# S5 outputs of a hybrid encoder as 64x64 matmul tiles by direction, with one copy of the states per tile

## The chip, the core and the metric

The kernel runs on one core of one Trainium2 chip. The metric is the time of one execution on the device in microseconds (us). TensorE (PE; its weight loads PEld) does the matmuls, VectorE (DVE) and ScalarE (ACT) the elementwise work, GpSimd (POOL) a little, and SyncE (SP) issues the DMAs.

## The reference

Two layers over 256 positions of width 2048. Each projects the stream, sends one half through a bidirectional complex-diagonal state space model (S5) in 64 groups of 16 channels with 64 states per direction, the other half through differential attention, and adds the projection of both back, followed by a LayerNorm. What matters here is the SSM:

```
for direction in range(2):
    y = y + s5_scan(uf, lam[direction], ..., b[direction], c[direction], reverse=(direction == 1))
# s5_scan: x_t = a * x_{t-1} + B u_t (complex, associative scan along time), returns
    einsum('bsgp,gcp->bsgc', x_re, c_re) - einsum('bsgp,gcp->bsgc', x_im, c_im)
```

The backward direction runs over time reversed, so its states come out in the opposite order of time.

## The kernel before

The weights (512 KB pieces) stream through SP's queue into `raw`, four deep. Each piece is split into a high part `wh` (a cast on ACT, L163) and a low part `wl` (a subtraction on VectorE, L165), and a **step** of 24 matmuls (`mm3`, L169 to L171) multiplies it. After every step the program calls `side`, which lets generators ("lanes") emit pieces of the SSM and of the attention heads; a scheduler then sets each engine's order when the program is built. All engines work through their order one instruction after the other.

The SSM runs in blocks of four positions: 64 blocks, the scan (`ssm_scan`, L552 to L555) over them on VectorE in `H`, whose innermost index is not the block. Partitions 0 to 63 of `H` hold the forward states, 64 to 127 the backward ones, whose blocks are in reversed order. `ssm_out` then goes through eight **tiles** o of eight groups. For a tile:

- `part` (L457, L459) builds the weights `w` from the table and C on VectorE, six operations;
- ACT copies the tile's states from `H` into `hcs` (names in the profile: `bh`), contiguous in blocks: the forward half as it is (L629), the backward half read in reverse (L630);
- `expand` (L571, `kw`) and `toep` (L578 on TensorE, L583 on ACT) make the local kernel `lt` inside a block;
- `outputs` (L592, L595) multiplies: per pair of groups pr, and for re and im, the two groups g2 with 128 states (both directions at once) by 64 outputs, and `lt` by U over 128 rows of which half are zero. One PSUM bank (`ss`, two in the pool) takes the tile; ACT copies it into `y4s` (`ub`, L599);
- every second tile `ready` stores y to memory; `load_y` and `split_y` read it back transposed, apply GELU (L617) and split it for the next matmuls.

Two tiles' `w` and two tiles' `hcs` exist at a time, and one `lt`. In both layers the tiles run beside the steps of the gate's projection (silu, L926) and of the output projection's first half. Parameters of the emission order (`BUDGET`, `PE_SHARE`, the costs that the lanes yield) are the same before and after.

Of the kernel before, what the change touches and what calls it, by code (L numbers as in the profile page):

```python
# [43 lines left out]
def kernel(  # L44
# [28 lines left out]
    V, A, PE, GP, SY = nc.vector, nc.scalar, nc.tensor, nc.gpsimd, nc.sync  # L73
    mult, add, sub = ALU.mult, ALU.add, ALU.subtract
# [4 lines left out]
    def T(shape, tag, bufs=1, dt=F32):  # L79
        return sb.tile(shape, dt, tag=tag, name=tag, bufs=bufs)  # L80

    def PS(shape, tag, bufs):
        return pp.tile(shape, F32, tag=tag, name=tag, bufs=bufs)

    def tp_bank(shape):
        return PS(shape, "tp", 2)

    def ss_bank(shape):
        return PS(shape, "ss", 2)
# [303 lines left out]

    cz = [T([128, 2, 8, 32], f"cz{i}") for i in range(2)]
    lt = [T([128, 8, 16, 4], f"lt{i}") for i in range(1)]
    for t in cz + lt:
        GP.memset(t, 0.0)

    class Ssm:
# [51 lines left out]
    def part(w, z, o, tr, M, m0, m1, op, r):  # L451

        gs = slice(8 * o, 8 * o + 8)
        x2 = T([128, 8, 16, 4], "x2")
        for dst, a, m in ((x2, tr + 1, m1), (w[:, r], tr, m0)):
            t = z.tab[:, a, 32 * o:32 * o + 32].rearrange("p (g j) -> p g j", j=4)
            V.tensor_tensor(dst, t.unsqueeze(2).to_broadcast([128, 8, 16, 4]),  # L457
                            M[:, m, gs, :].unsqueeze(3).to_broadcast([128, 8, 16, 4]), mult)
        V.tensor_tensor(w[:, r], w[:, r], x2, op)  # L459
# [98 lines left out]
    def ssm_out(l):  # L558
        z = ssm[l]
        y4s = {}  # L560
        hcs = T([128, 2, 2, 2, 4, 64], "bh")
        z.yT = z.yh = None
        ws = {}
        kws = {}

        def expand(o):

            kw = kws[o] = T([128, 2, 4, 16, 4], "kw")
            for q in range(2):
                w0 = z.kx[:, 2 * o + q, :, 3:7]  # L570
                A.copy(kw[:, q], bass.AP(w0.tensor, w0.offset, [w0.ap[0], [-1, 4], *w0.ap[1:]]))  # L571

        def toep(o):
            kw = kws[o]
            lp = tp_bank([128, 4, 64])
            for j in range(4):
                for q in range(2):
                    PE.matmul(lp[64 * q:64 * q + 64, j], lhsT=kw[:, q, j].rearrange("p c j -> p (c j)"), rhs=sel,  # L578
                              start=True, stop=True)
            for q in range(2):  # L580
                lv = lp[64 * q:64 * q + 64].rearrange("p j (a b c) -> p b a c j", a=2, b=2)
                for g2 in range(2):
                    A.copy(lt[0][64 * g2:64 * g2 + 64, 4 * q + g2:4 * q + 4:2], lv[:, g2])  # L583

        def outputs(o):
            yp = ss_bank([128, 4, 64])
            w, hc = ws[o], hcs[:, o % 2]
            for pr in range(4):
                halves = [(2 * pr + g2, yp[64 * g2:64 * g2 + 64, pr, :]) for g2 in range(2)]
                for ri in range(2):  # L590
                    for g, dst in halves:
                        PE.matmul(dst, lhsT=w[:, ri, g].rearrange("p c j -> p (c j)"),  # L592
                                  rhs=hc[:, g // 4, ri, g % 4, :], start=ri == 0, stop=False, skip_group_check=True)
                for g, dst in halves:
                    PE.matmul(dst, lhsT=lt[0][:, g].rearrange("p c j -> p (c j)"),  # L595
                              rhs=z.U[:, 4 * o + pr, :], start=False, stop=True, skip_group_check=True)
            if o % 2 == 0:
                y4s[o // 2] = T([128, 8, 64], "ub", 2)
            A.copy(y4s[o // 2][:, 4 * (o % 2):4 * (o % 2) + 4, :], yp)  # L599

        yv = y_dr.rearrange("(q g c) (j k) -> (g c j) q k", g=2, c=16, j=4)

        def ready(n):
            SY.dma_start(yv[:, 8 * n:8 * n + 8], y4s[n])

        def load_y():
            z.yT = T([128, 8, 256], "a8", 3)
            for n in range(2):
                SY.dma_start(z.yT[:, 4 * n:4 * n + 4],
                             y_dr[512 * n:512 * n + 512].rearrange("(o p) t -> p o t", p=128))  # L610

        def split_y():
            z.yh = T([128, 8, 256], "bh", 1, F32R)
            z.yl = T([128, 8, 256], "c8", 1, F32R)
            for c in range(4):
                cs = slice(2 * c, 2 * c + 2)
                A.activation(z.yT[:, cs], z.yT[:, cs], AF.Gelu_apprx_tanh)  # L617
            for c in range(4):
                cs = slice(2 * c, 2 * c + 2)
                A.copy(z.yh[:, cs], z.yT[:, cs])  # L620
                V.tensor_tensor(z.yl[:, cs], z.yT[:, cs], z.yh[:, cs].bitcast(F32), sub)

        for o in range(9):
            if o < 8:
                w = ws[o] = T([128, 2, 8, 16, 4], "w4", 2)
                part(w, z, o, 2, z.C, 0, 1, add, 0)
                hc = hcs[:, o % 2].rearrange("p q r g k -> p q (r g) k")
                src = z.H[:, 2 * o:2 * o + 2, 0:64].rearrange("p q k r g -> p q (r g) k")
                A.copy(hc[0:64], src[0:64])  # L629
                A.copy(hc[64:128], src[64:128, :, :, ::-1])  # L630
            if o > 0:
                outputs(o - 1)
                if o % 2 == 0:
                    ready(o // 2 - 1)
            if o < 8:
                expand(o)
            yield 1.8 if o < 8 else 0.0, 0, 2.5 if o else 0.0
            if o < 8:
                part(ws[o], z, o, 2, z.C, 1, 0, sub, 1)
                toep(o)  # L640
                yield 1.8, 0, 0.5
        load_y()
        yield 0.0, 2
        split_y()
        yield 2.0, 0
# [211 lines left out]
    for l in range(DEPTH):  # L857
# [8 lines left out]
        z = ssm[l]  # L866
# [30 lines left out]
        for hp in range(4):  # L897
            acc = block(hi, lo)
            while heads and heads[1].stage < 1:
                heads[1].one()  # L900
            rq = Lane(rotary_split(acc, 0.125, store, "q", (("qr", 1), ("xr", 2))), 0)
            rq.one()
            acc = block(hi, lo)
            finish(rq)
            rk = Lane(rotary_split(acc, 1.0, store, "k", (("kr", 1), ("xr", 2))), 0)
            rk.one()
            acc = block(hi, lo, tok_major=True)
            v = T([128, 2, 256], "v", 2)
            A.copy(v, acc)
            finish(rk)  # L910
            if hp == 0:
                l_out = Lane(ssm_out(l), 4, after=[l_scan])
            every += [Lane(head(hp, h, store["q"], store["k"], v, oT, neg, gsc), 1 + 0.1 * h) for h in range(2)]
            heads = every[-2:]
# [155 lines left out]
```

## Time and profile before

| | |
|---|---|
| median of 3 runs | 1031.38 us (1029.9 to 1032.72) |
| profiled execution | 1032.34 us, span 1030.6 us |
| TensorE, VectorE, ACT busy | 965.9, 773.8, 605.9 us |
| mean granted clock of TensorE | 0.985 |
| outputs stage, layer 0 and layer 1 | about 342 to 414 us and 806 to 889 us |

Busy time of TensorE counts matmuls from start to modelled end; consecutive ones overlap, so a row's busy time, not the mean of one matmul, says what a stream of them takes. "Idle before" in a row is the time in which the engine stood still ahead of it, with the instruction that ended the wait.

### The profile page before, as it was taken

What the parts mean: (1) busy time and instruction counts of PE and PEld (TensorE: products, weight loads), DVE (VectorE), ACT (ScalarE), POOL (GpSimd) and SP (SyncE); (2) the same over time, 40 slices, a digit from 0 to 9 for tenths busy, and PEclk for the clock granted to TensorE, in tenths of its full rate; (3) what the DMA queues carried; (4) which work ended last, traced back from release to release, by engine and by line L of the source; (5) the groups of instructions that cost most, each with busy time, mean ns of one, the idle gap of its engine ahead of it and who ended that gap; (6) DMA issues with size and microseconds to landing.
All of it is one profiled execution on the core that took longest, in us unless ns stands there. A gap on an engine that the chain in (4) does not pass through costs nothing.

```text
span 1030.6 us, 23623 instructions
## 1 busy us (share of the span) xinstructions
PE 965.9 (94%) x9792; PEld 932.7 (91%) x9792; DVE 773.8 (75%) x1310; ACT 605.9 (59%) x962; POOL 67.7 (7%) x104
## 2 busy tenths in 40 slices
PE   2899999999999988999889999999999998999995
PEld 2889988999999887999879989999999897999995
DVE  6875799899887666655588699988988566565676
ACT  2546586655575899444344585565566879843640
POOL 1000131010010000000010120010010000000001
PEclk9999999999999998999999999999999999999998
DMA  9897522455465524779965724545455443677973
GB/s 270 240 271 218 179 62 62 146 182 165 144 193 164 174 88 124 247 241 303 275 207 166 232 59 146 177 152 162 152 162 179 142 144 104 179 231 238 316 241 85
DMA packets 201867, 186.08 MB, mean 181 GB/s; under 512 B 38048, under 2 KB 194464, under 8 KB 201760
## 3 DMA queue, kind: packets, MB, share of 16 engines
q1 hardware_dynamic: 201760, 184.57, 58.4%
q8 instruction: 77, 1.26, 0.5%
q14 instruction: 30, 0.25, 0.1%
HBM read 169.21 MB, written 15.34 MB: 179 GB/s over the span
## 4 chain that ended last, share of the span: by engine, by line
PE 66%; ACT 11%; DMA 9%; DVE 7%; issue 3%; SPq 3%; POOL 1%; POOLq 0%; DVEq 0%; ACTq 0%
PE acc L169 19%; PE acc L170 18%; PE acc L171 18%; DMA raw<-in_w_out_dram 3%; ACT bh L630 3%; DVE wl L165 2%; ACT bh L629 2%; DMA rpart<-xr 2%; ACT wh L163 2%; PE ss L502 2%; PE sc L699 1%; PE tp L474 1%; PE ss L727 1%; PE ss L592 1%; DVE H L236 1%
## 5 line engine op out<-in xcount | busy, mean ns | idle before, releaser
L165 DVE TENSOR_TENSOR wl<-raw,wh 128x1024 fp32r<-128x1024 f32 x266 | 324.7, 1222 | 182.2 <-ACT wh L163 181.2
L163 ACT CAST wh<-raw 128x1024 fp32r<-128x1024 f32 x266 | 278.3, 1049 | 257.7 <-PE acc L170 109.6
L169 PE MATMUL acc<-xh,wh 128*128 128x256 f32 x1280 | 371.4, 291 | 2.4 <-ACT wh L163 1.3
L170 PE MATMUL acc<-xl,wh 128*128 128x256 f32 x1280 | 366.5, 286 | 3.0 <-DVE xl L254 2.9
L171 PE MATMUL acc<-xh,wl 128*128 128x256 f32 x1280 | 365.8, 286 | 1.8 <-DVE wl L165 1.8
L169 PEld LDWEIGHTS acc<-xh,wh 128*128 128x128 f32 x1280 | 246.3, 193 | 7.3 <-ACT xh L253 1.6
L170 PEld LDWEIGHTS acc<-xl,wh 128*128 128x128 f32 x1280 | 246.8, 193 | 4.9 <-DVE xl L254 4.0
L171 PEld LDWEIGHTS acc<-xh,wl 128*128 128x128 f32 x1280 | 246.7, 193 | 3.4 <-DVE wl L165 2.5
L169 PE MATMUL acc<-wh,xh 128*128 128x256 f32 x720 | 206.6, 287 | 2.7 <-ACT wh L163 1.9
L170 PE MATMUL acc<-wl,xh 128*128 128x256 f32 x720 | 205.7, 286 | 3.0 <-DVE wl L165 2.8
L171 PE MATMUL acc<-wh,xl 128*128 128x256 f32 x720 | 204.7, 285 | 0.0
L170 PEld LDWEIGHTS acc<-wl,xh 128*128 128x128 f32 x720 | 139.2, 193 | 4.1 <-DVE wl L165 4.0
L169 PEld LDWEIGHTS acc<-wh,xh 128*128 128x128 f32 x720 | 139.1, 193 | 3.7 <-ACT wh L163 2.5
L171 PEld LDWEIGHTS acc<-wh,xl 128*128 128x128 f32 x720 | 139.1, 193 | 0.1
L552 DVE TENSOR_TENSOR sa<-tab,H 128x256 f32<-128x256 f32 x126 | 53.1, 421 | 2.9 <-ACT H L505 0.7
L459 DVE TENSOR_TENSOR w<-w,x 128x512 f32<-128x512 f32 x64 | 45.5, 712 | 0.8
L709 ACT ACTIVATE e<-sc,mx 128x256 f32<-128x256 f32 x64 | 29.5, 476 | 19.3 <-DVE mx L703 19.3
L592 PE MATMUL ss<-bh,w 128*64 128x64 f32 x512 | 32.6, 236 | 6.5 <-ACT ub L599 6.5
L555 DVE TENSOR_TENSOR H<-sa 128x128 f32<-128x128 f32 x126 | 36.2, 287 | 2.1
L554 DVE TENSOR_TENSOR sa<-sa,H 128x128 f32<-128x128 f32 x126 | 36.1, 286 | 1.9
L505 ACT COPY H<-ss 128x512 f32<-128x512 f32 x32 | 33.9, 1176 | 4.1 <-PE ss L502 4.1
L171 PE MATMUL acc<-bh,wl 128*128 128x256 f32 x128 | 36.1, 282 | 0.0
(189 smaller groups left out, 1292.9 us busy)
## 6 DMA issues: line engine op xcount, KB each, us to landing
raw<-in_w_in_dram SPq DMA_DIRECT2D x192, 512.0 KB, 3.5
raw<-in_w_out_dram SPq DMA_DIRECT2D x64, 512.0 KB, 5.4
raw<-in_w_glu_dram SPq DMA_DIRECT2D x16, 512.0 KB, 5.4
xr<-xres SPq DMA_DIRECT2D x16, 256.0 KB, 3.5
rpart<-xr SPq DMA_DIRECT2D x16, 256.0 KB, 5.1
xr<-rpart SPq DMA_DIRECT2D x15, 256.0 KB, 4.6
xres<-H SPq DMA_DIRECT2D x14, 256.0 KB, 3.7
H<-in_x_dram SPq DMA_DIRECT2D x8, 256.0 KB, 5.9
```

The source lines that it names most:

```text
L163: A.copy(wh, raw)
L165: V.tensor_tensor(wl, raw, wh.bitcast(F32), sub)
L169: PE.matmul(o, lhsT=lh, rhs=rh, start=first, stop=False, skip_group_check=True)
L170: PE.matmul(o, lhsT=lh, rhs=rl, start=False, stop=False, skip_group_check=True)
L171: PE.matmul(o, lhsT=ll, rhs=rh, start=False, stop=last, skip_group_check=True)
L459: V.tensor_tensor(w[:, r], w[:, r], x2, op)
L505: A.copy(z.H[:, 2 * o:2 * o + 2, 1:65].rearrange("p q k r g -> p q (r g) k")[:, :, g2::2], ps[g2].rearrange("p q r g k -> p q (r g) k"))
L552: V.tensor_tensor(a.rearrange("p v q r g -> p v q (r g)"), lam, h.unsqueeze(1).to_broadcast([128, 2, 16, 8]), mult)
L554: V.tensor_tensor(a[:, 0], a[:, 0], nx, add)
L555: V.tensor_tensor(nx, a[:, 0], a[:, 1, :, ::-1, :], add)
L592: PE.matmul(dst, lhsT=w[:, ri, g].rearrange("p c j -> p (c j)"), rhs=hc[:, g // 4, ri, g % 4, :], start=ri == 0, stop=False, skip_group_ch ...
L630: A.copy(hc[64:128], src[64:128, :, :, ::-1])
```

## The change

Three things change in `ssm_out`, and one at the start.

1. The states are copied by one instruction for all 128 partitions, none reversed.
2. `outputs` multiplies by 64x64 tiles: row half d is the direction, column half g2 the group of the pair. Each direction has a PSUM bank of its own, and the backward states are read in reverse by the matmul. The `lt` matmuls take the diagonal quadrants alone, 64 rows each, so that the zeros in `lt` are no longer read and are no longer written at the start. A tile has 40 matmuls, not 24.
3. The result is ACT's copy of the one bank, to which VectorE adds the other.

```diff
-    for t in cz + lt:
+    for t in cz:
         GP.memset(t, 0.0)
...
         def outputs(o):
-            yp = ss_bank([128, 4, 64])
+            yps = [ss_bank([128, 4, 64]) for _ in range(2)]
             w, hc = ws[o], hcs[:, o % 2]
+            halves = [slice(0, 64), slice(64, 128)]
             for pr in range(4):
-                halves = [(2 * pr + g2, yp[64 * g2:64 * g2 + 64, pr, :]) for g2 in range(2)]
                 for ri in range(2):
-                    for g, dst in halves:
-                        PE.matmul(dst, lhsT=w[:, ri, g].rearrange("p c j -> p (c j)"),
-                                  rhs=hc[:, g // 4, ri, g % 4, :], start=ri == 0, stop=False, skip_group_check=True)
-                for g, dst in halves:
-                    PE.matmul(dst, lhsT=lt[0][:, g].rearrange("p c j -> p (c j)"),
-                              rhs=z.U[:, 4 * o + pr, :], start=False, stop=True, skip_group_check=True)
+                    for d in range(2):
+                        for g2 in range(2):
+                            g = 2 * pr + g2
+                            h = hc[halves[d], g // 4, ri, g % 4, :]
+                            PE.matmul(yps[d][halves[g2], pr, :],
+                                      lhsT=w[halves[d], ri, g].rearrange("p c j -> p (c j)"),
+                                      rhs=h[:, ::-1] if d else h,
+                                      start=ri == 0, stop=ri == 1 and d != g2, skip_group_check=True)
+                for g2 in range(2):
+                    PE.matmul(yps[g2][halves[g2], pr, :],
+                              lhsT=lt[0][halves[g2], 2 * pr + g2].rearrange("p c j -> p (c j)"),
+                              rhs=z.U[halves[g2], 4 * o + pr, :], start=False, stop=True, skip_group_check=True)
...
-            A.copy(y4s[o // 2][:, 4 * (o % 2):4 * (o % 2) + 4, :], yp)
+            y4 = y4s[o // 2][:, 4 * (o % 2):4 * (o % 2) + 4, :]
+            A.copy(y4, yps[0])
+            V.tensor_tensor(y4, y4, yps[1], add)
...
-                A.copy(hc[0:64], src[0:64])
-                A.copy(hc[64:128], src[64:128, :, :, ::-1])
+                A.copy(hc, src)
```

In the changed kernel the lines further down have other numbers: L597 and L602 are the matmuls of the states and of `lt`, L608 the copy, L609 the addition, L639 the copy of the states, L627 the GELU, L935 the silu.

The order of ACT, layer 0, one tile and the beginning of the next, before (`bh` is `hcs`, `ub` the tile's result):

```order
L629 COPY bh<-H 64x1024 [waits PE_49]
L630 COPY bh<-H 64x1024
L599 COPY ub<-ss 128x256 [waits PE_49]
L583 COPY lt_73<-tp 64x2x64 [waits PE_49,Activation_49]
L583 COPY lt_73<-tp 64x2x64 [waits Activation_49] x3
L571 COPY kw<-kx 128x256 [waits Activation_49]
L571 COPY kw<-kx 128x256
L163 CAST wh<-raw 128x1024 [waits DMAHW7_49,DVE_49,PE_49]
```

And the same place now:

```order
L639 COPY bh<-H 128x1024 [waits PE_49]
L608 COPY ub<-ss 128x256 [waits PE_49]
L583 COPY lt_73<-tp 64x2x64 [waits PE_49,Activation_49]
L583 COPY lt_73<-tp 64x2x64 [waits Activation_49] x3
L571 COPY kw<-kx 128x256 [waits Activation_49]
L571 COPY kw<-kx 128x256
L163 CAST wh<-raw 128x1024 [waits DMAHW7_49,DVE_49,PE_49]
```

One copy is gone; the rest stands as it stood.

The order of VectorE in layer 0, between two weight subtractions, before (w and x are made by `part`):

```order
L457 TENSOR_TENSOR w_4725<-tab,c_1061 128x512 [waits PE_49]
L457 TENSOR_TENSOR w_4725<-tab,c_1061 128x512
L459 TENSOR_TENSOR w_4725<-w_4725,x_4726 128x512 [waits DVE_49]
L457 TENSOR_TENSOR x_4762<-tab,c_1061 128x512 [waits DVE_49]
L459 TENSOR_TENSOR w_4725<-w_4725,x_4762 128x512 [waits DVE_49]
L457 TENSOR_TENSOR x_4780<-tab,c_1061 128x512 [waits DVE_49]
L165 TENSOR_TENSOR wl<-raw,wh 128x1024 [waits DMAHW7_49,PE_49,Activation_49]
```

And now:

```order
L457 TENSOR_TENSOR w_4740<-tab,c_1060 128x512 [waits PE_49]
L457 TENSOR_TENSOR w_4740<-tab,c_1060 128x512
L459 TENSOR_TENSOR w_4740<-w_4740,x_4741 128x512 [waits DVE_49]
L609 TENSOR_TENSOR ub<-ub,ss 128x256 [waits PE_49,Activation_49]
L457 TENSOR_TENSOR x_4794<-tab,c_1060 128x512 [waits DVE_49]
L459 TENSOR_TENSOR w_4740<-w_4740,x_4794 128x512 [waits DVE_49]
L457 TENSOR_TENSOR x_4812<-tab,c_1060 128x512 [waits DVE_49]
L165 TENSOR_TENSOR wl<-raw,wh 128x1024 [waits DMAHW7_49,PE_49,Activation_49]
```

The addition stands between the two halves of the weights of the tile two further on.

The order of TensorE around tiles 1 and 2 of layer 0, before (`w_4641` is tile 1, `w_4725` tile 2):

```order
L592 MATMUL ss<-bh,w_4641 64x64 x4
L169 MATMUL acc<-xh_142,wh 128x256
L170 MATMUL acc<-xl_143,wh 128x256
L171 MATMUL acc<-xh_142,wl 128x256 [waits DVE_49]
L592 MATMUL ss<-bh,w_4725 64x64 [waits DVE_49,Activation_49]
L595 MATMUL ss<-a_170,lt_73 64x64 [waits Activation_49] x2
L592 MATMUL ss<-bh,w_4641 64x64 x4
L595 MATMUL ss<-a_170,lt_73 64x64 x2
```

And at tile 2 now (`w_4740`):

```order
L597 MATMUL ss<-bh,w_4740 64x64 [waits Activation_49]
L597 MATMUL ss<-bh,w_4740 64x64
L597 MATMUL ss<-bh,w_4740 64x64 [waits DVE_49]
L597 MATMUL ss<-bh,w_4740 64x64
L602 MATMUL ss<-a_169,lt_73 64x64 [waits Activation_49]
L597 MATMUL ss<-bh,w_4740 64x64
L597 MATMUL ss<-bh,w_4740 64x64 [waits DVE_49]
L597 MATMUL ss<-bh,w_4740 64x64 x3
```

A tile's matmuls now stand together, and their first ones wait for both engines that read the banks. Counted over the whole order, 24 matmuls to a step, 8.96 steps lay between the first and the last tile's outputs in layer 0 and 8.46 in layer 1; now 6.67 in both, one step between neighbouring tiles up to the last.

## Rows read from the trace of the kernel before

**Rows 1.** The page: an engine's busy time, share of the span, instructions.

```profile
PE 965.9 (94%) x9792; PEld 932.7 (91%) x9792; DVE 773.8 (75%) x1310; ACT 605.9 (59%) x962; POOL 67.7 (7%) x104
```

**Rows 2.** Windows: stretch, length, busy PE, PEld, DVE, ACT, POOL (instructions), clock, DMA, GB/s.

```profile
349.50:413.40 63.90, 54.05 (x754) 50.10 (x752) 39.94 (x52) 59.59 (x89) 0.00 (x0) 0.95 0.39 120
810.00:815.00 5.00, 2.74 (x24) 2.54 (x23) 0.00 (x0) 4.95 (x6) 0.00 (x0) 1.00 0.00 1
815.00:820.00 5.00, 5.00 (x36) 4.45 (x37) 3.96 (x4) 4.95 (x11) 0.00 (x0) 0.66 0.30 90
837.50:888.20 50.70, 45.26 (x658) 42.26 (x655) 33.15 (x44) 48.15 (x70) 0.00 (x0) 0.97 0.34 104
...
413.40:470.00 56.60, 56.60 (x476) 56.60 (x476) 34.84 (x35) 27.14 (x33) 0.00 (x0) 1.00 0.79 245
888.20:1000.00 111.80, 111.80 (x936) 111.80 (x937) 68.49 (x75) 57.19 (x70) 0.00 (x0) 1.00 0.82 262
```

**Rows 3.** Timeline of ACT in layer 0: start, duration, instruction, idle before it.

```profile
357.20 2.17 ACT L629 COPY bh<-H 64x1024 f32<-64x1024 f32 x1 [0.51 <-PE ss L592]
359.38 2.14 ACT L630 COPY bh<-H 64x1024 f32<-64x1024 f32 x1
361.54 0.37 ACT L599 COPY ub<-ss 128x256 f32<-128x256 f32 x1
...
364.56 2.19 ACT L629 COPY bh<-H 64x1024 f32<-64x1024 f32 x1
```

**Rows 4.** Timeline of VectorE over one tile of layer 0.

```profile
364.68 1.22 DVE L165 TENSOR_TENSOR wl<-raw,wh 128x1024 fp32r<-128x1024 f32 x1 [2.75 <-ACT wh L163]
365.82 1.28 DVE L457 TENSOR_TENSOR w<-tab,c 128x512 f32<-128x512 f32 x2
...
369.20 0.69 DVE L457 TENSOR_TENSOR x<-tab,c 128x512 f32<-128x512 f32 x1
372.10 1.22 DVE L165 TENSOR_TENSOR wl<-raw,wh 128x1024 fp32r<-128x1024 f32 x1 [2.21 <-ACT wh L163]
```

**Rows 5.** Groups of instructions by form: busy us, mean ns, idle before.

```profile
L502 PE MATMUL ss<-a,H 64*64 64x64 f32 x1024 | 26.9, 224 | 0.8 <-ACT H L505 0.7
...
L505 ACT COPY H<-ss 128x512 f32<-128x512 f32 x32 | 33.9, 1176 | 4.1 <-PE ss L502 4.1
...
L1000 DVE TENSOR_TENSOR H<-xr,acc 128x256 f32<-128x256 f32 x8 | 3.3, 411 | 2.4 <-DMA xr<-rpart 1.9 <-PE acc L171 0.4
```

**Rows 6.** Timeline of TensorE at four places of layer 0.

```profile
349.56 0.68 PE L578 MATMUL tp<-cst,kw 128*64 128x64 f32 x16
351.57 0.39 PE L169 MATMUL acc<-xh,wh 128*128 128x256 f32 x1 [1.32 <-ACT wh L163]
...
352.83 0.39 PE L171 MATMUL acc<-xh,wl 128*128 128x256 f32 x1 [0.76 <-DVE wl L165]
...
360.52 0.28 PE L171 MATMUL acc<-xh,wl 128*128 128x256 f32 x1
360.73 0.45 PE L592 MATMUL ss<-bh,w 128*64 128x64 f32 x8
...
412.02 0.34 PE L595 MATMUL ss<-a,lt 128*64 128x64 f32 x4
...
413.33 0.38 PE L171 MATMUL acc<-wh,xl 128*128 128x256 f32 x1
```

**Rows 7.** VectorE, SP's queue and ACT around the first load of y; DMA landing.

```profile
391.07 1.29 DVE L932 TENSOR_TENSOR xl<-a,xh 128x512 fp32r<-128x512 f32 x2
...
392.39 0.37 SPq L609 DMA_DIRECT2D a<-y_dr  x1
...
398.51 1.28 ACT L617 ACT_TABLE_LOAD   x1
...
400.86 2.18 ACT L629 COPY bh<-H 64x1024 f32<-64x1024 f32 x1
...
a<-y_dr SPq DMA_DIRECT2D x4, 512.0 KB, 4.7
```

## The prediction

> **What bounds the kernel now.** I read the page first: TensorE is busy 94% of the span [rows 1], so a change pays only where TensorE waits. Then the windows, to find such places near the change. While the SSM outputs are made, ACT is busy 59.6 of 63.9 us in layer 0 and 48.2 of 50.7 in layer 1, while TensorE has 9.9 and 5.4 us idle and a granted clock under 1 [rows 2]; a third place lies in layer 1 at 810 to 820 us: 2.3 us idle, then a clock of 0.66 with 36 matmuls where 5 us at full clock hold 42. Behind the stages, at 413 to 470 and 888 to 1000 us, TensorE is 100% busy, a matmul per 0.12 us: what the stages give back is kept, since nothing there waits for a fixed time.
>
> Then the timelines, engine by engine, for one tile (one o of outputs). ACT goes from one L629 to the next in 7.36 us without a gap, and two copies of 2.2 and 2.1 us (L629, L630) are over half of it [rows 3]. VectorE needs 5.21 us per tile (364.68 to 369.89) and then waits 2.21 for ACT's cast [rows 4]. So ACT sets the pace and the other two follow.
>
> **The copy.** 16 tiles, one copy each instead of two. The two forms that exist, forward and reversed, take about the same time on 64 partitions, and each partition's 1024 elements stay as they are; I take 2.16 us (359.38 to 361.54) for the 128-partition copy. Bounds: nothing more, or twice this if partitions counted, which would undo the saving; but the 128-partition H<-ss copy with half as many strided elements takes 1.18 us [rows 5], so the first. ACT per tile: 7.36 - 2.16 = 5.20 us.
>
> **The add.** VectorE gets 16 additions of 128x256 with a PSUM operand. The nearest row, L1000, takes 0.41 us [rows 5]; with a gap of 0.04, 0.45. VectorE per tile: 5.21 + 0.45 = 5.66 us. It is now the longest.
>
> **The matmuls.** A tile had 24 of 128x64, 1.31 us from first to next acc (412.02 to 413.33) [rows 6]. It gets 32 on four quadrants and 8 of the lt diagonal. The same shape with the same reversed reading is in the trace: 1024 of L502 in 26.9 us, 26 ns each, so four run at a time [rows 5]. 32 x 26 ns is 0.84 us; the lt matmuls fill two quadrants, 8 x 53 = 0.42. Sum 1.27 us, no change worth counting. Bounds: 26 ns each throughout (1.05), or one at a time at four times that, 107 ns (4.3), a rival below. One thing speaks against it: the tile's outputs are now 64x64, toep behind them still 128x64, the step 128x128, so there is one more change of shape per tile. Rows bound it: acc to L592 takes 0.21 us from issue to issue where 0.12 is usual [rows 6], so 0.1 us, 1.6 us for 16 tiles if it showed.
>
> The Trainium skill, TensorEngine Tiling (Array Packing), section Tiling Modes, says that a changed tiling mode, not merely another tile, drains TensorE. By that each of the 16 extra changes costs a drain; with the row's 0.1 us the sum would be 1.6 us worse where TensorE sets the pace, and nothing where VectorE does.
>
> **TensorE per tile.** The order now puts exactly one weight step (24 matmuls) between two tiles where it was about 1.29. A step is 24 x 0.12 = 2.88 us, outputs 1.3, toep 0.68 [rows 6], changes of shape 0.3: 5.2 us.
>
> **What waits newly.** outputs takes both ss banks, so its first matmuls wait for ACT's copy and VectorE's add of the tile before. What is queued behind them on TensorE is toep and the next step; for those ACT and VectorE wait in turn. The add stands behind the first half of w (1.93 us), which waits for outputs anyway, and TensorE has toep and a step (3.5 us) meanwhile: w 1.93, add 0.45, about 0.2 of signalling is 2.6, so covered as long as VectorE is on time. Its 5.66 then is the pace.
>
> **Layer 0 as a timetable.** Before, outputs(0) ends at 357.20 (L629 starts on it) and outputs(7) at 413.33. In front, the first two tiles' copies hold up the weight casts: TensorE waits 1.32 and 0.76 us [rows 6]. ACT now is 4.3 us earlier there, so outputs(0) ends at 355.1. To outputs(4): 5.20, then three times 5.66: 377.3. Next the four xl subtractions (two rows of two, 1.2 us each pair from start to start): 5.66 + 2.4, 385.4. Next ACT has a table load and two gelus, 2.35 us (398.51 to 400.86, where L629 starts): 5.20 + 2.35. These gelus wait for the first half of y, whose load needs the buffer that the last xl frees (before: xl ends 392.36, load issued 392.39, landing 4.7 us later) [rows 7]; formerly it landed just before ACT came, now ACT comes earlier. By the order, ACT has only lt, kw and a cast (some 2.7 us) between, less what VectorE lags: I price the wait at 3 us (0 to 3.6). outputs(6) ends at 395.9. The last tile has no copy of H but a table load and a silu (3.02 + 1.9): 400.8. Fewer steps lie between the first and the last tile now, 6.67 and not 8.96 by the two orders; 2.29 x 2.88 = 6.6 us are still due: 407.4 against 413.3. Gain 5.9 us.
>
> **Layer 1.** At 810 the four copies stand before L737, for whose output TensorE waits; 4.3 us less on ACT clear the 2.26 idle and the six matmuls lost to the clock: 3.0 us. outputs(0) ended at 837.5, now 834.5. Then 5.20, five times 5.66, and a last one of 4.2 (0.67 step): 872.2. Owed: 8.46 - 6.67 = 1.79 steps, 5.2 us: 877.4 against 888.1. Gain 10.7 us.
>
> Sum 16.6. For signals between three engines that are now nearly equal I take off 0.15 us for each of 14 tiles: 14.5. The profiled execution took 1032.3, so 1017.8; the median of the runs shown is 1.0 below it: **1017 us**. Removing lt's zeroing touches the start of POOL alone: nothing. Four more table loads (1.28 each) fall behind the stages mostly, where ACT has half its time free.
>
> **Rivals.**
> *Fuller recovery.* VectorE's lag is hidden by working ahead (pace 5.2, 8 tiles x 0.46 = 3.7), no wait for y (3), no signalling (2.1): gain 23.5, 1008 us. For it: x of the next tile is already computed ahead. Against: VectorE is in order and w needs the outputs. 15%.
> *The two banks bite.* If the add regularly stands behind a weight subtraction (1.15 us from start to start), half of it per tile, 14 x 0.6 = 8 us, stays on the path: gain about 6, 1025 us. 14%. If the whole of it does, 16 us, nothing is left: about 1031 us, 5%.
> *Slower.* Quadrant matmuls run one at a time (the lt diagonals or the accumulation over ri breaking the overlap, which L502 doesn't have since each of its results is one matmul): 40 x 107 ns = 4.3 us, TensorE per tile 8.1, (8.1 - 5.66) x 14 = 34 us: 1017 + 34 = 1051. It decides from a pace of 5.66 + 1.05 = 6.7 us, some 70 ns per matmul; two at a time (53 ns) costs 0.35 us per tile, 5 us. 4%.
> *The copy doesn't shrink* (4.3 us on 128 partitions): ACT's tile as long as before, 1031 us; held under the 5% above.
>
> **How the numbers follow.** The forecast, a gain of 9 to 20 us (1012 to 1023), has 62%; fuller 15, half 14, nothing 5, slower 4. The likeliest gives 1017. Reaching into the neighbours on both sides until about 2 in 10 are out, with the wait for y at 0 to 3.6 and the signals at 0 to 0.6: 1008 to 1025. About 0.3% (3 us) is what a measurement can tell from no change: faster 0.91, same 0.05, slower 0.04.
>
> **What would show it.** Right: one ACT copy of 128x1024 at 2.1 to 2.2 us per tile; ACT and VectorE both over 90% busy in the stage with a tile every 5.5 to 6 us; quadrant matmuls at about 30 ns; the add at 0.4 us; the idle at 812 us gone; a wait of ACT's L627 for y in layer 0. Wrong: TensorE waiting for the add longer than a few tenths per tile, the quadrant matmuls over 60 ns each, or new idle time behind the stages that takes the gain back.

## The result, and the profile after

The changed kernel takes 1014.06 us (median of 4 runs, 1013.52 to 1015.72) against 1031.61 (1029.9 to 1032.72) for the kernel before: a ratio of 0.9825, 95% interval 0.9800 to 0.9849. The profiled execution took 1013.52 us, its span is 1011.7 us. The forecast was 1017 us, in a range of 1008 to 1025.

The page of the changed kernel answers to [rows 1]; the last line is the chain that ended last, by engine.

```profile
span 1011.7 us, 24655 instructions
PE 960.5 (95%) x10304; PEld 928.7 (92%) x10304; DVE 777.7 (77%) x1326; ACT 576.6 (57%) x950; POOL 72.4 (7%) x103
...
PE 70%; DMA 13%; DVE 7%; ACT 4%; SPq 3%; issue 2%; POOL 1%; POOLq 0%; DVEq 0%; ACTq 0%
```

TensorE's busy time fell by 5.4 us and the rest of the span, in which it waits, from 64.7 to 51.2 us. ACT lost 29.3 us of work, VectorE got 3.9 more.

The groups by form of the changed kernel, for the four lines of the change (busy us, mean ns, idle before):

```profile
L639 ACT COPY bh<-H 128x1024 f32<-128x1024 f32 x16 | 34.7, 2182 | 1.5 <-PE ss L597 1.1
L597 PE MATMUL ss<-bh,w 64*64 64x64 f32 x1024 | 29.0, 231 | 3.6 <-ACT ub L608 3.6
L602 PE MATMUL ss<-a,lt 64*64 64x64 f32 x256 | 25.0, 224 | 0.0
L609 DVE TENSOR_TENSOR ub<-ub,ss 128x256 f32<-128x256 f32 x16 | 6.7, 417 | 6.1 <-ACT ub L608 5.9
```

One copy of 128x1024 takes what one of 64x1024 took [rows 3]. The x1024 of L597 shows what the prediction misread in L502's row: the code issues 32 matmuls per tile, 512 in all, and the trace has 1024. An fp32 matmul stands in it twice.

The windows of the changed kernel (columns as in [rows 2]): layer 0's stage, the stretch behind it, the place at 810, layer 1's stage.

```profile
349.50:397.80 48.30, 44.72 (x954) 42.38 (x953) 36.81 (x54) 42.60 (x78) 0.00 (x0) 0.96 0.46 138
404.40:470.00 65.60, 63.20 (x518) 61.84 (x517) 35.80 (x36) 30.38 (x36) 0.00 (x0) 1.00 0.80 247
810.00:815.00 5.00, 5.00 (x44) 5.00 (x43) 1.91 (x2) 2.09 (x2) 0.00 (x0) 1.00 0.81 253
815.00:820.00 5.00, 5.00 (x44) 5.00 (x43) 2.37 (x3) 2.54 (x3) 0.00 (x0) 1.00 0.55 160
818.00:864.30 46.30, 46.30 (x987) 44.02 (x986) 36.35 (x53) 38.22 (x71) 0.00 (x0) 1.00 0.46 137
```

In layer 1's stage TensorE now has no gap at all and its full clock; before it was idle for 5.4 of 50.7 us. The idle time and the low clock at 810 are gone (by the table below the place now begins some 6 us earlier; TensorE is busy without a gap and at its full clock from 799 to 870 us). Layer 0's stage keeps 3.6 us of idle time. The stretch behind it, without a gap before, now has 2.4 us of gaps.

To see where the time came from I numbered the 272 subtractions of the weight split (L165, VectorE), from 0 on, in both timelines and took the difference of the starts of the same one. Each weight step has one, so this is the lead in work done, whatever the order between:

| n-th L165 | place | before, at us | lead of after |
|---|---|---|---|
| 88 | ahead of layer 0's stage | 342.0 | 0.1 |
| 104 | behind it | 425.9 | 9.5 |
| 128 | output projection of layer 0 | 501.4 | 3.8 |
| 212 | ahead of the 810 place | 805.8 | 6.2 |
| 216 | behind it | 822.7 | 11.3 |
| 230 | behind layer 1's stage | 890.9 | 18.1 |
| 271 | end | 1005.1 | 18.7 |

Layer 0's stage gives 9.4 us, 3.3 go again, the 810 place gives 5.1, layer 1's stage 6.8 and the rest 0.6. Inside a stage the two orders differ, so a single number depends on the place: around number 104 the lead is 5.9 (103) and 10.5 (105). The same count on TensorE's 6528 weight matmuls (L169 to L171), which sees TensorE's own work, gives leads of 0.1, 8.9, 4.6, 6.2, 11.3 and 18.7 us at about 341, 420, 500, 806, 823 and 895 us of the kernel before. So the parts are good to about 1 us.

### The profile page after: what moved, and what is told of

The parts are those of the page before. It is cut to its first block, busy times and chain, and to the rows that moved or that the text cites. A ratio compares the mean times of both kernels' runs of the same rounds, so it can differ in the third digit from the quotient of the medians.

```text
span 1011.7 us, 24655 instructions
## 1 busy us (share of the span) xinstructions
PE 960.5 (95%) x10304; PEld 928.7 (92%) x10304; DVE 777.7 (77%) x1326; ACT 576.6 (57%) x950; POOL 72.4 (7%) x103
## 4 chain that ended last, share of the span: by engine, by line
PE 70%; DMA 13%; DVE 7%; ACT 4%; SPq 3%; issue 2%; POOL 1%; POOLq 0%; DVEq 0%; ACTq 0%
PE acc L169 19%; PE acc L170 19%; PE acc L171 19%; DMA rpart<-xr 5%; DMA raw<-in_w_out_dram 4%; DVE wl L165 2%; PE ss L502 2%; PE ss L597 2%; DMA raw<-in_w_glu_dram 2%; ACT wh L163 2%; PE tp L474 1%; PE sc L708 1%; PE ss L736 1%; SPq L428 1%; DVE H L236 1%
## 5 line engine op out<-in xcount | busy, mean ns | idle before, releaser
L165 DVE TENSOR_TENSOR wl<-raw,wh 128x1024 fp32r<-128x1024 f32 x266 | 324.7, 1222 | 148.4 <-ACT wh L163 146.6
L169 PE MATMUL acc<-xh,wh 128*128 128x256 f32 x1280 | 370.7, 290 | 1.1 <-ACT xh L253 0.9
L171 PE MATMUL acc<-xh,wl 128*128 128x256 f32 x1280 | 364.3, 285 | 0.7 <-DVE wl L165 0.7
L169 PEld LDWEIGHTS acc<-xh,wh 128*128 128x128 f32 x1280 | 245.3, 192 | 6.1 <-ACT xh L253 1.6
L171 PEld LDWEIGHTS acc<-xh,wl 128*128 128x128 f32 x1280 | 245.7, 192 | 1.8 <-DVE wl L165 1.1
L169 PE MATMUL acc<-wh,xh 128*128 128x256 f32 x720 | 206.0, 287 | 4.7 <-ACT wh L163 2.2
L171 PE MATMUL acc<-wh,xl 128*128 128x256 f32 x720 | 204.1, 284 | 0.0
L169 PEld LDWEIGHTS acc<-wh,xh 128*128 128x128 f32 x720 | 138.5, 193 | 5.8 <-ACT wh L163 2.4
L171 PEld LDWEIGHTS acc<-wh,xl 128*128 128x128 f32 x720 | 138.4, 192 | 0.0
L459 DVE TENSOR_TENSOR w<-w,x 128x512 f32<-128x512 f32 x64 | 45.5, 711 | 0.8
L171 PE MATMUL acc<-bh,wl 128*128 128x256 f32 x128 | 36.4, 284 | 0.9 <-DVE wl L165 0.9
L742 POOL TENSOR_SCALAR ms<-ms 128x2 f32<-128x2 f32 x16 | 16.1, 1008 | 286.8 <-ACT on L741 286.8
```

The lines of the kernel that those rows point to most:

```text
L165: V.tensor_tensor(wl, raw, wh.bitcast(F32), sub)
L169: PE.matmul(o, lhsT=lh, rhs=rh, start=first, stop=False, skip_group_check=True)
L171: PE.matmul(o, lhsT=ll, rhs=rh, start=False, stop=last, skip_group_check=True)
```

## The experiments

The ratios are to the kernel before, run beside each on the same chip, with the 95% interval. "Idle" is span minus TensorE's busy time, both from the page of the profiled execution.

| run | median us | ratio | span | PE busy | idle |
|---|---|---|---|---|---|
| before | 1031.61 | 1 | 1030.6 | 965.9 | 64.7 |
| e0_after | 1011.86 | 0.9789 (0.9764 to 0.9814) | 1011.0 | 960.0 | 51.0 |
| e1_copy_only | 1010.81 | 0.9749 (0.9692 to 0.9806) | 1007.8 | 957.3 | 50.5 |
| e2_tiles_only | 1044.62 | 1.0106 (1.0065 to 1.0146) | 1042.1 | 970.4 | 71.7 |
| e3_no_add | 1017.79 | 0.9822 (0.9776 to 0.9868) | 1019.8 | 964.0 | 55.8 |
| e4_xr4 | 1007.64 | 0.9740 (0.9714 to 0.9767) | 1005.8 | 959.4 | 46.4 |
| e5_before_xr4 | 1028.05 | 0.9942 (0.9917 to 0.9967) | 1027.1 | 968.2 | 58.9 |
| e6_pool_half_xr4 | 1024.08 | 0.9883 (0.9852 to 0.9914) | 1019.9 | 957.4 | 62.5 |
| e7_copy_xr4 | 1002.73 | 0.9696 (0.9664 to 0.9728) | 999.5 | 952.3 | 47.2 |
| e8_four_banks_xr4 | 1008.35 | 0.9738 (0.9713 to 0.9763) | 1008.6 | 959.4 | 49.2 |
| e9_tiles_four_banks | 1043.02 | 1.0068 (1.0043 to 1.0093) | 1042.3 | 971.6 | 70.7 |

The theory was that the time comes from ACT's second copy alone, and that part of it is lost again behind layer 0's stage through the residual blocks; the rivals, that the tile shape gains by itself, or that the add and the two banks take back several us.

**e1: the copy alone.** The kernel before, with one copy:

```
-                A.copy(hc[0:64], src[0:64])
-                A.copy(hc[64:128], src[64:128, :, :, ::-1])
+                A.copy(hc, src)
```

> The kernel before with the two copies of the states replaced by the one 128-partition copy, unreversed; matmuls of 128x64, one bank and ACT's copy as before. It leaves out the reversal of the backward states, so its output is not the reference's. Theory (ACT's second copy held the stages): ACT's tile is 5.2 us, VectorE's 5.2, and the time falls as much as with the whole change, to 1010 to 1017 us. Rival (the quadrant matmuls give the time): no less than 1026 us.

0.9749: the copy alone gives the whole gain, and by the middle of the ratios more than the whole change (the intervals overlap, and the two were not measured beside each other). ACT's copies start at 353.76, 359.00, 364.24, 369.16 and 374.29 us, 5.13 us apart on the mean, where the changed kernel's outputs are 5.51 apart.

**e2: the tiles alone.** The changed kernel with the two copies back, and a forward reading:

```
-                                      rhs=h[:, ::-1] if d else h,
+                                      rhs=h,
...
-                A.copy(hc, src)
+                A.copy(hc[0:64], src[0:64])
+                A.copy(hc[64:128], src[64:128, :, :, ::-1])
```

> The changed kernel with ACT's two 64-partition copies put back, the second reversed, so that the matmul reads forward; quadrant matmuls, two banks and the addition stay. Theory: ACT's tile is 7.4 us again and sets the pace, the addition and the banks lie beside it: 1028 to 1035 us. Rival (the quadrant matmuls give the time): 1014 to 1020 us.

Missed: the tiles alone make the kernel 1.06% slower. The waits of TensorE in layer 0's stage (350 to 413.4 us), first in the kernel before, then here (us in all, times, longest):

```profile
PE ss L595 <- ACT lt L583: 4.5, 2, 2.3
PE ss L592 <- ACT ub L599: 3.2, 4, 1.4
PE acc L169 <- ACT wh L163: 1.3, 1, 1.3
PE acc L171 <- DVE wl L165: 0.8, 1, 0.8
```

```profile
PE ss L597 <- ACT ub L608: 13.3, 5, 6.7
PE acc L169 <- ACT wh L163: 1.3, 1, 1.3
PE acc L171 <- DVE wl L165: 0.8, 1, 0.8
```

15.4 us of waits instead of 9.8. With two banks a tile's first matmul waits until ACT has read the banks of the tile ahead (L608), and that copy stands on ACT behind this tile's 4.3 us of state copies, in one place (408.25 us) also behind two table loads. A tile's outputs also take 2.00 us from the first to toep (363.58 us and on), where most tiles before took 1.45 to 1.54. And the clock was 0.83 in 350 to 360 us, where it was 1.00 before.

**e9: e2 with four banks.** Odd tiles use the two banks that hold attention's scores elsewhere.

```
+            if o % 2:
+                sc = PS([128, 2, 8, 64], "sc", 1)
+                yps = [sc[:, d, 0:4] for d in range(2)]
+            else:
+                yps = [ss_bank([128, 4, 64]) for _ in range(2)]
```

> The 64x64 tiles with the two ScalarE copies of before, and four PSUM banks for the outputs instead of two. Theory (with two banks the outputs of a tile wait for ScalarE's copy of the outputs of the tile ahead, which stands behind the 4.3 us of state copies of this tile; TensorE waited 13.3 us there in layer 0's stage against 9.8 in the kernel before): 4 to 10 us under the two-bank form, 1034 to 1040 us, ratio 1.000 to 1.006. Rival (the 10 us come from where the steps fall: the clock that halved at 353.8 us and two more table loads): no difference, 1042 to 1046 us, ratio 1.009 to 1.012.

Between the two: 1.0068, with an interval that overlaps e2's. The wait for the copy of the outputs (L608, here L612) falls from 13.3 to 1.8 us, but 8.2 us of waits for lt (L583) come in its place, so all waits are 12.1 us in the same window. By the middle of the two ratios the banks are 0.4 of e2's 1.1%, but since the intervals overlap this isn't shown; how the loss divides among the banks, the longer outputs, the clock and the order stays open.

**e3: without the add.** L609 is left out, and with it the backward half of the outputs.

```
-            V.tensor_tensor(y4, y4, yps[1], add)
```

> The changed kernel without VectorE's addition, so that the backward direction's bank is left out of the output. Theory: VectorE's tile falls from 5.5 to 5.2 us, but TensorE needs 5.5 itself, so the time falls by 0 to 3 us to 1011 to 1014. Rival (the add and its bank are on the path in every tile): 0.33 us or more for 14 tiles, with the wait for the bank 5 to 10 us less, 1004 to 1009.

0.9822, so no gain is seen against the changed kernel's 0.9789 or 0.9825, and the rival's 5 to 10 us aren't there. That the add costs nothing at all isn't shown: without it the order has moved, ACT's wait for y at the gelu has grown to 3.99 us (it is 1.37 with the add), and the interval (0.9776 to 0.9868) leaves room for some us either way.

**e0, e4, e5, e7: four residual buffers.** e0 is the changed kernel again, beside e4. In the first half of the output projection each block xr is loaded into one of two buffers, added to, and stored to rpart; the load of block n+2 waits on SP's queue for the store of block n to land, and the weight loads queue behind it. e4 is the changed kernel with four buffers, e5 the kernel before with them, e7 e1 with them (reversal left out as in e1):

```
-            xr = T([128, 2, 256], "xr", 2)
+            xr = T([128, 2, 256], ("xr", "xr", "qs", "sh")[cb % 4], (2, 2, 1, 1)[cb % 4])
```

> The changed kernel as it is, for comparison on the same chip: 1014 us, within 0.3%.

> The changed kernel with four buffers for the residual in the output projection's first half (xr, xr, qs, sh in turn) and not two. In layer 0 the lead over the kernel before falls from 9.5 to about 5 us behind the stage. Theory (the round trip store of rpart, landing, load of the next xr in SP's queue gives it back): the round trip is broken, 3 to 5 us less, 1009 to 1011 us. Rival (the DMA engines themselves are full there): within 1 us of 1014.

> The kernel before with the same four buffers. Theory: there the round trip lagged behind TensorE too, by 5 us at the end of the block, so 1 to 4 us less, 1027 to 1030 us. Rival (DMA engines full): within 1 us of 1031.5.

> The matmuls of the kernel before with one copy of the states on 128 partitions, unreversed (the backward states are read in the wrong order, so the reversal is left out), and four residual buffers. Theory (the recovered time of the stage is partly given back through the store and load of the residual blocks, with either form of the matmuls): 2 to 4 us under the one-copy kernel's ratio of 0.9749, so 1005 to 1009 us, ratio 0.970 to 0.973. Rival (the give-back was peculiar to the 64x64 tiles): no difference, 1010 to 1012 us, ratio 0.975.

The changed kernel gains 4.2 us by it, from 1011.86 to 1007.64 (no run of either lies among the other's), which lies in the 3 to 5 us of the theory. The kernel before gains 0.58%, some 6 us and more than the 1 to 4 expected; its 1028.05 us fits the forecast only because the kernel before took 1035.05 beside it. From e1 to e7 it is some 0.5% (0.9749 to 0.9696, not measured beside each other). SP's waits between 395 and 520 us for these stores, in the kernel before, the changed kernel and e4 (where `qs` and `sh` are the two further buffers):

```profile
SPq L936 <- DMA rpart<-xr: 15.2, 5, 5.1
```

```profile
SPq L945 <- DMA rpart<-xr: 26.7, 6, 5.1
```

```profile
SPq L945 <- DMA rpart<-xr: 7.8, 2, 5.0
SPq L945 <- DMA rpart<-qs: 4.3, 1, 4.3
SPq L945 <- DMA rpart<-sh: 3.7, 1, 3.7
```

The changed kernel waits 11.5 us longer there than before. Four buffers shorten the waits and don't end them: 15.8 us in e4, and 5.6 in e5 where the kernel before has 15.2. The chain that ended last in the changed kernel runs through them (start us, us, what; pieces under 0.1 us are left out):

```profile
416.54 6.06 DMA rpart<-xr
422.61 0.37 SPq L945
423.07 0.42 SPq L150
423.54 6.09 DMA rpart<-xr
429.65 0.37 SPq L945
430.11 0.42 SPq L150
430.58 5.71 DMA rpart<-xr
```

A block per 7.0 us: the store, the issue of the load that waited for it, the issue of a weight load, the next store. This is the wait with a fixed time behind the stage. But the buffers gained the kernel before about as much, and a second profile of the changed kernel (e0) loses 0.7 us between L165 number 104 and 212, not 3.3 (9.7 and 9.0 us of lead). So four buffers are shown to be worth some 4 to 6 us in each of the two kernels; that the round trip costs more because the stage gives more is seen in SP's waits and not in the times.

**e8: four banks for the changed kernel**, with e4's buffers and e9's edit.

> The changed kernel with four residual buffers, and with four PSUM banks for the outputs instead of two (odd tiles use the two banks that attention's scores have elsewhere). Theory A (with one copy on ScalarE the two banks cost little: TensorE waited 3.6 us in all for the copy of the outputs in layer 0's stage): 1005 to 1008 us, ratio 0.972 to 0.974, at most 2 us under the run with four buffers alone (0.974). Theory B (the banks are what the tiles still cost against the one copy alone, 3 to 4 us): 1003 to 1005 us, ratio 0.970 or less.

0.9738 against 0.9740: the banks cost nothing that can be measured once ACT has one copy. Layer 0's tiles do come closer: outputs start at 357.11, 362.26, 367.17 and 372.08 us, 4.99 apart, against 5.51 in e4. But most of this is work put off, not saved: between two tiles TensorE does 20 matmuls of a step in e8 (369.49 to 372.08 us) and 24 in e4 (366.00 to 369.06), 0.47 us of the 0.52. By L165 the lead over the kernel before is 13.9 us against 8.6 at number 104, 13.7 against 11.0 at 212, and 23.5 against 24.3 at the end.

**e6: GpSimd takes the reversed half.** The matmuls of before, with e5's buffers:

```
-                A.copy(hc[64:128], src[64:128, :, :, ::-1])
+                GP.tensor_copy(hc[64:128], src[64:128, :, :, ::-1])
```

> The matmuls of the kernel before, but GpSimd copies the reversed half of the states and ScalarE the forward half alone; four buffers for the residual blocks in both layers. Theory (it is the second 2.16 us of copying on ScalarE that held the tile, and nothing else): GpSimd's copies of 64x256 elements took 0.71 to 0.81 us, so 64x1024 should take about 2.8 to 3.3 us, well inside a tile of 5.2 us; the time is that of one copy with four buffers, 1006 to 1011 us, ratio 0.971 to 0.977. Rival: GpSimd takes over 5 us for this copy, or slows VectorE beside it, and becomes what each tile waits for; the time is then 1018 to 1032 us, ratio 0.985 or more.

The rival won, for its second reason: 0.9883. GpSimd's copy takes 2.45 us, less than priced, but VectorE stands still meanwhile. Both engines' timelines around 360 us:

```profile
360.47 2.07 POOL L630 COPY bh<-H 64x1024 f32<-64x1024 f32 x1 [2.43 <-PE ss L595]
```

```profile
359.83 0.69 DVE L457 TENSOR_TENSOR x<-tab,c 128x512 f32<-128x512 f32 x1
360.56 2.53 DVE L459 TENSOR_TENSOR w<-w,x 128x512 f32<-128x512 f32 x1
363.12 0.69 DVE L457 TENSOR_TENSOR x<-tab,c 128x512 f32<-128x512 f32 x1
```

L459 takes about 0.69 us elsewhere; here it starts 0.09 us behind GpSimd's copy and ends 0.55 us after it. Over the span VectorE is busy 802.9 us where it is 773.2 in e7: 1.86 us more for each of the 16 copies, and TensorE waits 6.6 us for w (L459) in layer 0's stage. The Trainium skill's page SBUF — State Buffer, section "SBUF: two separate sides", says that VectorE and GpSimd share a pair of ports as an exclusive lock, which a VectorE operation with two SBUF inputs needs as well when the GpSimd operation reads SBUF; these rows agree with it. So e6 doesn't test whether ACT's second copy was all that held the tile; e1 is the run that does.

## Why the prediction was right, point by point

**ACT's copy (right).** 2.16 us predicted, 2.18 measured (L639), and e1 shows that this term carries the gain. ACT needed 5.15 us from one copy to the next where it had work all the time (366.07 to 371.22; 5.20 predicted); the copies before are 5.47 and 5.87 us apart, the second with a silu between:

```profile
366.07 2.21 ACT L639 COPY bh<-H 128x1024 f32<-128x1024 f32 x1
368.17 0.38 ACT L608 COPY ub<-ss 128x256 f32<-128x256 f32 x1
...
371.22 2.20 ACT L639 COPY bh<-H 128x1024 f32<-128x1024 f32 x1
```

**VectorE sets the pace at 5.66 (wrong in the engine, near in the size).** VectorE's tile, beside [rows 4]:

```profile
360.10 1.23 DVE L165 TENSOR_TENSOR wl<-raw,wh 128x1024 fp32r<-128x1024 f32 x1 [0.27 <-ACT wh L163]
361.24 1.28 DVE L457 TENSOR_TENSOR w<-tab,c 128x512 f32<-128x512 f32 x2
362.44 0.68 DVE L459 TENSOR_TENSOR w<-w,x 128x512 f32<-128x512 f32 x1
363.04 0.41 DVE L609 TENSOR_TENSOR ub<-ub,ss 128x256 f32<-128x256 f32 x1
363.37 0.68 DVE L457 TENSOR_TENSOR x<-tab,c 128x512 f32<-128x512 f32 x1
...
365.58 1.23 DVE L165 TENSOR_TENSOR wl<-raw,wh 128x1024 fp32r<-128x1024 f32 x1
```

The add occupies 0.33 us from its start to the next, not 0.45, and this period is 5.48 us. TensorE's is 5.51 (outputs start at 358.38, 363.89, 369.40 and 374.90) and has no gap in it; in the same three periods VectorE is busy for 5.16 to 5.37 us and ACT for 5.25 to 5.41. So all three stand nearly level, and TensorE is the one that doesn't wait. That 5.66 lies near 5.51 is luck: TensorE's tile was put at 5.2, and what it lacked is the next term.

**The outputs at 1.27 us (mis-sized, and with them TensorE's tile of 5.2).** "1024 of L502 in 26.9 us, 26 ns each" is 26 ns per record. The code of L502 issues 512 matmuls, and each stands twice in the trace, as those of L597 do: 53 ns per matmul. So the 32 matmuls of a tile are 64 records: 64 x 26 ns = 1.7 us, not 0.84. Measured: L597 is busy for 29.0 us in 16 tiles, 1.81 us each, in which the lt matmuls run as well. A tile's outputs with the lt matmuls among them take 1.56 us up to toep in layer 0's first tile and 1.83 in the four behind it:

```profile
353.15 0.46 PE L597 MATMUL ss<-bh,w 64*64 64x64 f32 x16
...
363.89 0.45 PE L597 MATMUL ss<-bh,w 64*64 64x64 f32 x8
364.17 0.22 PE L602 MATMUL ss<-a,lt 64*64 64x64 f32 x1
...
365.51 0.28 PE L602 MATMUL ss<-a,lt 64*64 64x64 f32 x2
365.72 0.69 PE L578 MATMUL tp<-cst,kw 128*64 128x64 f32 x16
```

The quadrants do run side by side, but not at the rate that was taken: the 40 matmuls of a tile in 1.83 us are 46 ns each, and 39 in the first tile; the prediction's 1.27 us would be 32. That lies between "26 ns each throughout" and the prediction's own case "two at a time (53 ns)", which it held for unlikely and priced at 5 us; one at a time didn't come. In the first tile 16 records start in the 0.28 us ahead of the first of L602, in the next ones 8: by their order four matmuls of L597 stand ahead of the first L602 there, where the code writes eight. Whether this order makes them slower was not tried.

A tile of the old shape took 48 records in 1.45 us (355.65 to 357.10 in the kernel before), 60 ns per matmul. (The 1.31 us that the prediction read for it, from 412.02 on, hold 40 of the 48 records; eight had run from 408.33 on.) So the new shape is quicker per matmul, but a tile now has 64 + 16 = 80 records, and has them in a stage that TensorE bounds. This fits the 0.4% between e0 and e1 and between e4 and e7 (0.9740 against 0.9696, 4.5 us): by an estimate from these rows, 0.38 us more for 14 tiles are some 5 us. It isn't shown apart, since the two runs of a pair were not measured beside each other and differ in the banks and the add as well.

**One more change of shape (right).** From the start of the last two L602 records to L578 are 0.21 us, the same as from acc to L592 in [rows 6]. The Trainium skill, TensorEngine Tiling (Array Packing), section Tiling Modes, has a drain there; the trace agrees, with a start some 0.1 us later than in a stream of one shape, the prediction's bound.

**Two banks, and the add, are covered (right but for one place).** TensorE waits 3.6 us in all of layer 0's stage for L608, most of it in one wait of 2.9 us behind the gelus, which the prediction didn't have, and nothing in layer 1's; e8 finds no time in the banks, and e3 none in the add as far as it goes. e2 shows the condition: with 7.4 us of work for ACT per tile the same two banks make TensorE wait 13.3 us.

**The wait for y (right in kind, 1.37 us for 3).**

```profile
385.23 1.28 ACT L627 ACT_TABLE_LOAD   x1 [1.37 <-DMA a<-y_dr]
```

**Layer 0's gain, 5.9 us (mis-sized: 9.4, or 8.8 counted on TensorE).** The first copy started at 354.73 us, 0.4 before the time given. The tiles were shorter than 5.66 and the wait for y by 1.6; the last tile's cast L630 starts at 397.79, and the prediction had its outputs end at 400.8: 3 us later, which is the difference.

**Layer 1's gain, 10.7 us (11.9).** The 810 place gave 5.1 us instead of 3.0, layer 1's stage 6.8 instead of 7.7. The table's 5.1 has some work in it that the order does earlier or later, so the two are best read as one.

**0.15 us per tile for signals (not needed).** No row stood behind this term, and no run shows it: TensorE has no gap in layer 1's stage.

**"What the stages give back is kept" (failed in part).** 0.7 to 3.3 us of lead go behind layer 0's stage, where TensorE had been 100% busy [rows 2]. A fixed time does stand there, the store of a block, hidden so far: busy 100% of a stretch says that nothing was late before, not that nothing will be. New idle time behind the stages is the one of the prediction's own signs of being wrong that showed.

In sum the lead is 18.7 us where 14.5 were forecast: layer 0's stage gave 3.5 more, layer 1 1.2, the signals took none of their 2.1, 3.3 went again and 0.6 came behind the stages. So the mechanism was right (ACT's second copy held the stages), but 1014 lies so near to 1017 partly by luck: TensorE's longer outputs stood in for VectorE's pace, and what was given back made up for gains that were put too low. (The sum of the rival of a fuller recovery is 23.3 us, not 23.5; nothing hangs on it.)

## What to carry to other kernels

Count the records of a row against the calls in the code before a mean of it is multiplied: an fp32 matmul here is two. A change that frees an engine and loads another should be taken apart on the chip: here one edit (a copy over twice the partitions) was worth 2.5% (e1; with four buffers 2.5% from e5 to e7), and the reshaping that makes its result right cost, by the middle of the ratios, about 0.4% of it back. When a stall goes, look behind it for a round trip of fixed length through memory (here two buffers and a 6 us store); more buffers paid in the kernel before and in the changed one, and the changed kernel with four of them, at 0.974, beats both.

## What the runs showed of the hardware that was not expected

A GpSimd copy of 64x1024 elements held up a VectorE operation on two SBUF operands for nearly its whole length: 2.53 us instead of 0.69, beside a copy of 2.07. GpSimd's 7% of busy time was no free capacity in this stage.

ACT's copy with strided elements took 2.18 us on the mean for 128 partitions (L639), and 2.18 and 2.13 us for 64, forward and reversed (L629, L630): partitions and direction were free.

Forty fp32 matmuls of 64x64 on four quadrants took 1.56 to 1.83 us, 39 to 46 ns each, where 24 of 128x64 took 1.45 us, 60 each: a third to a half more matmuls in the same time, not twice as many.
